# Layer two of a two-layer trunk: memory attention moved to its front, one sample step per pair of heads, twelve gates at its end

## The chip, the cores and the metric

The kernel runs on one core of a Trainium2 chip. The metric is the device time of one execution in microseconds (us). The median of three runs of the kernel before is 906.5 us (905.1 to 909.17).

## The reference, cut to what matters

One inference step of a two-layer decoder trunk of width 2048, for two groups of requests that share the weights: a prompt of 256 tokens and 8 samples of one token, so 264 columns in all. Layer one mixes tokens by sliding-window attention, layer two by a gated linear recurrence (HGRN2) with 12 heads of 128x128 state. Each layer also has 4 heads of attention over a memory of 256 rows, a SiLU gate over all 16 blocks of 128, an output projection and a LayerNorm.

```python
q, f, iv, mq, g = split(h @ w_in)                 # layer two: 12, 12, 12, 4, 16 blocks of 128
fg = lb + (1 - lb) * sigmoid(f);  k = 1 - fg;  q = silu(q)
S_t = fg_t * S_{t-1} + k_t v_t^T;  o_t = q_t S_t  # per head; S starts at 0 (prompt) or at the state (samples)
o = o * rsqrt(mean(o^2) + 1e-6) * norm_w
mem_o = softmax(mq @ mk^T / sqrt(128)) @ mv       # prompt: mk, mv computed here; samples: from caches
y = (concat(o, mem_o) * silu(g)) @ w_out
h = LayerNorm(alpha * h + y)
```

The outputs are both hidden states, the memory keys and values, the window of keys and values, and the recurrent states of the prompt and of the 8 samples.

## The kernel before, in words

**Units.** The work is a list of some 170 units (class `Stream`, lines 58 to 131). A unit is one 128x2048 block of weights, cache or state in float32 (1 MB; a state unit of the kernel before has half of it) and a function that uses it. For each unit the block is loaded into one of four `raw` buffers by the sync engine's queue (`load`, line 79), then split into two float16 halves in one of four `hl` buffers: the high part by ScalarE (line 97), the low part by VectorE (line 98). Loads and splits run up to four units ahead. A block with `whole=True` keeps its `raw` buffer until its unit has run.

**Projections.** `proj` (line 308) multiplies a unit's block with the 264 columns: 16 chunks of 128 rows, three float16 passes each (lines 303 to 305), 48 matmuls of 264 columns into a PSUM bank of tag `pj`, of which there are two. The result is read out of its bank by ScalarE and VectorE, and only then the bank is free for a later projection.

**Layer two before.** For each pair of heads the units are f, f, v, v, then for each head q, half a block of sample state, and for heads 0 to 7 the gate. Then come the four memory queries mq, eight cache units c_mk and c_mv with gates 8 to 13 between, the other gates, and the 16 output projections o.

**Side steps.** When the second q of a pair is projected, `hq_unit` (line 1009) hands the pair to a generator, `hg_side` (line 1064), which goes on one step after each unit: `after(i)` calls `pump(1)`. A pair's chain computes scores in levels of 1, 2, 4, ..., 64 tokens. `prepare` (ScalarE line 1079, VectorE lines 1080, 1084 and 1087) makes the operands of a level, `products` the matmuls hs, `keep` (line 1111) copies them under a mask. After level 64 come the copy of its scores (1147), the transposes pk (1152) with the copy kn (1154), the state product pu (1158), the output hpo (1169 to 1171), its copy osb (1173), squares (1177), the row means rms (1182), Ln and Exp with a table load each (1183, 1186), and the scaled output (1189). A gate that was projected early lies in `mix` and is multiplied in at once (`gate_by`, lines 728 to 730); otherwise `gate_unit` does so when its turn comes, and pumps the chain until the head is done. The memory heads have such generators too (`memp_side`).

**Sample state.** `state_unit` (line 1197) computes a head's sample outputs from the split state (matmuls hos), then updates the float32 state in its `raw` buffer: matmuls vb spread the values over partitions, ScalarE scales by the forget gate (line 1237, 8 times a head), VectorE adds (line 1238), and the buffer is written back as out_ss by GpSimd's queue.

**Order.** The code is written for a tile framework that places the instructions of each engine in one order, by its own estimate of when each could start; each engine then runs its row strictly in that order, waiting on semaphores. PSUM tags matter for it: `pj` two banks, `pt` two (pk, pu, vb and the transposes hvp and hvr), `sc` two (hs, rms), `pv` and `ms` one each. `hvt`, the copy of a pair's v, has one buffer.

Of the kernel before, what the change touches and what calls it, by code (L numbers as in the profile page):

```python
# [18 lines left out]
P = 128  # L19
NC = 16  # L20
# [13 lines left out]
NG1 = 8  # L34
# [23 lines left out]
class Stream:  # L58


    def __init__(self, nc, pool, nraw, nsplit):
        self.nc, self.pool = nc, pool
        self.nraw, self.nsplit = nraw, nsplit
        self.units = []
        self.raw = {}
        self.hl = {}

# [37 lines left out]
    def run(self, pump):  # L105
# [11 lines left out]
        for i in range(n):  # L117
# [8 lines left out]
            while free < prepped and (free <= i or self.units[free][5]):  # L126
                free += 1
# [7 lines left out]
def trunk_kernel(  # L135
# [75 lines left out]
    bias_s = pm.tile([P, 2, NQ], F32, name="bias_s")  # L211

# [770 lines left out]
    def f_unit(h):  # L983
        def fn(hl):
# [4 lines left out]
            pt = proj(hl, xhl, T, f"f{h}")  # L989
            i = h % 2  # L990
            if i == 0:
# [3 lines left out]
                cur["ks8"] = p1.tile([P, 2, TS], F32, tag="ks8", name=f"ks8{h}", bufs=2)  # L995
            fg, kk, ks8 = cur["fg"][:, i], cur["kk"][:, i], cur["ks8"][:, i]
# [6 lines left out]
            nc.vector.tensor_scalar_mul(ks8, kk, 1.0 / (SA * SK))  # L1003
# [5 lines left out]
    def hq_unit(h):  # L1009
        def fn(hl):  # L1010
# [5 lines left out]
            if h % 2 == 1:  # L1016
                side.append(hg_side(h // 2, cur["q"], cur["vn"], cur["fg"], cur["qk"]))
# [23 lines left out]
    def hv_rows(h, vt, vs, vn, vr):  # L1041
# [7 lines left out]
        nc.vector.tensor_copy(vr[:, i], p16)  # L1049
# [14 lines left out]
    def hg_side(pi, q, vn, fg, qk):  # L1064
# [119 lines left out]
        for i, sq in enumerate(sqs):  # L1184
# [3 lines left out]
            scaled = mix[:, h] if h >= NG1 else sq  # L1188
# [3 lines left out]
            if h < NG1:  # L1192
                gate_by(sq, mix[:, h], h)
# [3 lines left out]
    def state_unit(h):  # L1197
        def fn(hl):
            p1 = H["p"]
            pi, i = h // 2, h % 2  # L1200
            raw = stream.raw[state_at[h]][:, : TS * P]
            R = raw.rearrange("p (b v) -> p b v", b=TS)
            v = hl[:, :, : TS * P].rearrange("p s (b v) -> p s b v", b=TS)
            vr, fgs, ks8 = cur["vr"][:, i], cur["fg"][:, i, TP:T], cur["ks8"][:, i]
            qs, vts = (cur[n][:, i, TP:T] for n in ("q", "vt"))
            ks = cur["kk"][:, i]
            if i == 0:
                osb[pi] = p1.tile([P, 2, T], F32, tag="osb", name=f"osb{pi}", bufs=2)
            qk = p1.tile([P, TS], F32, tag="qk", name=f"qk{h}", bufs=2)
# [5 lines left out]
            nc.scalar.activation(qkh[:, 0], qk, AF.Copy)
            nc.vector.tensor_tensor(qkh[:, 1], qk, qkh[:, 0], op=ALU.subtract)
            nc.scalar.activation(qfh[:, :, 0], qf, AF.Copy)
            nc.vector.tensor_tensor(qfh[:, :, 1], qf, qfh[:, :, 0], op=ALU.subtract)
            po = bank("ms", 1, f"hos{h}")
            pov = po[:, : 2 * TS].rearrange("p (b s) -> p b s", s=2)  # L1220
            for b in range(TS):
                mm(pov[:, b], v[:, 0, b], qfh[:, b], start=True, stop=False)
                mm(pov[:, b, 0:1], v[:, 1, b], qfh[:, b, 0:1], start=False, stop=True)
            pq = po[:, 2 * TS : 3 * TS]
# [48 lines left out]
    while late:  # L1273
        g1(late.popleft())
# [158 lines left out]
```

## Time and profile before

| | |
|---|---|
| runs | 905.1, 906.5, 909.17 us; median 906.5 |
| the profiled execution | 906.08 us |
| its span, first to last instruction | 904.3 us |
| mean granted TensorE clock | 0.994 |
| TensorE, VectorE, ScalarE busy | 98%, 78%, 64% |
| HBM | 180.03 MB read, 17.22 MB written, 218 GB/s over the span |

All durations in this text are from that one execution. PE is TensorE, PEld its weight load, DVE VectorE, ACT ScalarE, POOL GpSimd, SP the sync engine; L303 is line 303 of the kernel. The chain of waits follows the work that ended last backwards; in the rows of groups the columns are busy time, mean nanoseconds of one instruction, and the idle time of the engine before them with what ended it. By the first and last start of their matmuls, f of layer two begins at 420.1 us, the last hq is at 701.7, the memory queries end at 729.2, the sample memory attention (mso) at 783.3, the gates at 799.8, and the output projections at 893.1.

### The profile page before, as it was taken

To read this page: it belongs to the slowest core of one execution; us is meant where nothing else is said; L and a number is where in the kernel's file an instruction comes from. 1 tells how busy PE (TensorE), PEld (TensorE's weight loads), DVE (VectorE), ACT (ScalarE), POOL (GpSimd) and SP (SyncE) were. 2 spreads that over 40 slices of the span, in tenths; PEclk is the share of its full clock that TensorE was granted. 3 is DMA by queue.
4 is the path that set the end of the run, shared out by engine and by line. 5 is a ranking of instruction groups with operands and counts; after the bars stand their busy time and mean duration, and the time that the engine had idled before them with its cause. 6 is when DMAs were issued, how large, how long until landed. Compare 5 with 4: busy or idle time off the path is not lost.

```text
span 904.3 us, 21814 instructions
## 1 busy us (share of the span) xinstructions
PE 886.6 (98%) x9281; PEld 762.9 (84%) x9281; DVE 701.5 (78%) x1230; ACT 582.4 (64%) x982; POOL 34.9 (4%) x68
## 2 busy tenths in 40 slices
PE   9999999999999999999999999999999999799996
PEld 6888889678888888876888888898888888688996
DVE  6879877669886666697687887979788989678736
ACT  6767776657664444476766877777777585858415
POOL 1100010000000000002000000000000000000000
PEclk9999999999999999999999999999999999899999
DMA  9998566557785555556374655827454878456303
GB/s 340 392 353 317 188 245 209 188 208 265 262 333 192 187 192 203 207 198 214 127 292 137 216 201 174 299 101 260 160 215 164 303 283 308 172 207 244 130 2 97
DMA packets 37853, 198.67 MB, mean 220 GB/s; under 512 B 4555, under 2 KB 10732, under 8 KB 17532
## 3 DMA queue, kind: packets, MB, share of 16 engines
q1 hardware_dynamic: 33024, 181.55, 56.3%
q0 software_dynamic: 4688, 15.67, 4.6%
q8 instruction: 72, 1.18, 0.5%
q14 instruction: 25, 0.20, 0.1%
q10 hardware_dynamic: 44, 0.07, 0.0%
HBM read 180.03 MB, written 17.22 MB: 218 GB/s over the span
## 4 chain that ended last, share of the span: by engine, by line
PE 77%; DVE 8%; ACT 6%; DMA 6%; issue 3%; SPq 0%; ACTq 0%; DVEq 0%
PE o L303 5%; PE o L305 5%; PE o L304 5%; PE g L305 5%; PE g L303 5%; PE g L304 5%; DVE hl L98 4%; ACT hl L97 2%; PE hv L305 2%; PE hv L303 2%; PE hv L304 2%; DMA raw<-in_w_in 2%; PE hq L303 2%; PE hq L305 2%; PE hq L304 2%
## 5 line engine op out<-in xcount | busy, mean ns | idle before, releaser
L98 DVE SCALAR_TENSOR_TENSOR hl<-raw,hl 128x2048 f16<-128x2048 f32 (+2 forms) x168 | 358.6, 2138 | 82.0 <-ACT hl L97 81.0
L97 ACT ACTIVATE hl<-raw 128x2048 f16<-128x2048 f32 (+2 forms) x168 | 299.2, 1784 | 97.8 <-PE o L305 45.4
L305 PEld LDWEIGHTS <-hl 128*128 128x128 f16 (+2 forms) x2048 | 197.4, 98 | 31.8 <-DVE hl L98 2.9
L303 PEld LDWEIGHTS <-hl 128*128 128x128 f16 (+2 forms) x2048 | 197.3, 98 | 30.6 <-issue 2.2
L304 PEld LDWEIGHTS <-hl 128*128 128x128 f16 (+2 forms) x2048 | 197.4, 98 | 30.3 <-issue 2.2
L305 PE MATMUL g<-xhl,hl 128*128 128x264 f16 x512 | 142.0, 277 | 2.4 <-DVE hl L98 2.4
L303 PE MATMUL g<-xhl,hl 128*128 128x264 f16 x512 | 141.9, 277 | 0.0
L304 PE MATMUL g<-xhl,hl 128*128 128x264 f16 x512 | 141.9, 277 | 0.0
L303 PE MATMUL o<-mix,hl 128*128 128x264 f16 x384 | 105.4, 276 | 0.8 <-DVE xres L747 0.8
L304 PE MATMUL o<-mix,hl 128*128 128x264 f16 x384 | 105.8, 276 | 0.0
L305 PE MATMUL o<-mix,hl 128*128 128x264 f16 x384 | 105.7, 276 | 0.0
L303 PE MATMUL q<-xhl,hl 128*128 128x264 f16 x192 | 53.0, 276 | 1.0 <-DVE kst L251 1.0
L303 PE MATMUL f<-xhl,hl 128*128 128x264 f16 x192 | 52.9, 276 | 0.4 <-DVE mvhl L251 0.4
L305 PE MATMUL hv<-xhl,hl 128*128 128x264 f16 x192 | 53.0, 276 | 0.0
L303 PE MATMUL hq<-xhl,hl 128*128 128x264 f16 x192 | 53.0, 276 | 0.0
L304 PE MATMUL hq<-xhl,hl 128*128 128x264 f16 x192 | 53.0, 276 | 0.0
L305 PE MATMUL hq<-xhl,hl 128*128 128x264 f16 x192 | 53.0, 276 | 0.0
L304 PE MATMUL hv<-xhl,hl 128*128 128x264 f16 x192 | 53.0, 276 | 0.0
L303 PE MATMUL hv<-xhl,hl 128*128 128x264 f16 x192 | 53.0, 276 | 0.0
L304 PE MATMUL q<-xhl,hl 128*128 128x264 f16 x192 | 53.0, 276 | 0.0
L305 PE MATMUL q<-xhl,hl 128*128 128x264 f16 x192 | 53.0, 276 | 0.0
L304 PE MATMUL f<-xhl,hl 128*128 128x264 f16 x192 | 52.9, 276 | 0.0
(338 smaller groups left out, 1858.4 us busy)
## 6 DMA issues: line engine op xcount, KB each, us to landing
raw<-in_w_in SPq DMA_DIRECT2D x88, 1024.0 KB, 6.4
raw<-in_w_o SPq DMA_DIRECT2D x32, 1024.0 KB, 5.0
raw<-in_w_mk SPq DMA_DIRECT2D x8, 1024.0 KB, 4.9
raw<-in_w_mv SPq DMA_DIRECT2D x8, 1024.0 KB, 4.9
raw<-in_c_mk SPq DMA_DIRECT2D x8, 1024.0 KB, 5.1
raw<-in_c_mv SPq DMA_DIRECT2D x8, 1024.0 KB, 7.0
raw<-in_state SPq DMA_DIRECT2D x12, 512.0 KB, 5.4
out_ss<-raw POOLq DMA_DIRECT2D x12, 512.0 KB, 5.5
```

The costliest lines, as they stand in the source:

```text
L97: hi = self.nc.scalar.activation(hl[:, 0, s], raw[:, s], AF.Copy, scale=scale)
L98: lo = self.nc.vector.scalar_tensor_tensor(hl[:, 1, s], raw[:, s], scale, hl[:, 0, s], op0=ALU.mult, op1=ALU.subtract)
L303: mm(out, lhs(0), rhs(0), start=start, stop=False)
L304: mm(out, lhs(0), rhs(1), start=False, stop=False)
L305: return mm(out, lhs(1), rhs(0), start=False, stop=stop)
```

## The change

The list of units of layer two is written anew.

- The four memory queries come right behind f of head 0, then the eight cache units, each with one projection of pair 0 (or gates 0 and 1, or f of pair 1) behind it.
- A pair's two half state units become one of 1 MB, for both heads. The small operations on it are joined (128x16 in place of 128x8), the update of its second head is put off to the next unit (`later`), and the stream holds its `raw` buffer one unit longer (`longer`).
- From pair 2 on a pair has seven units: f, f, v, v, q, q, state; gate 2 follows pair 1's state, gate 6 that of pair 3. Only gates 0, 1, 2 and 6 are early. The other twelve are last, with those of heads 10 and 11 at the very end, ahead of the output projections.
- `after` pumps no step behind a cache unit, two behind f of head 1 and v of head 0, one behind f of head 2, else one, or two where more than one generator is waiting (after state unit 0).
- `apart=True`: q of head 0 in layer one and f of head 0 in layer two use the `pv` bank and do all passes with high weights first.
- The constant `sel` carries the factor 1/(SA*SK), so the multiply into ks8 (line 1003 before) is gone.
- `LATER` is empty: the code for late state updates (`fetch`, `late_update`, `with_update`, `kept`) never runs.

What the engines' rows become at three places follows. Line numbers of the new kernel are a few higher (L307 to L309 are the passes, L1088 and L1092 in `prepare`, L1213 the scaling).

TensorE, pair 3's last levels, before: hs3_64 is level 64 of pair 3, hv9 and hq8 are projections of heads 9 and 8.

```order
L305 MATMUL hv9_8935<-xhl_93,hl123_8684 128x264
...
L303 MATMUL hs3_64_8987<-qk16_2_5655 128x64
...
L303 MATMUL hq8_9018<-xhl_93,hl124_8779 128x264
...
L304 MATMUL hs3_64_8987<-qk16_2_5655 128x64
...
L1152 MATMUL pk3_9001<-ident_66,qk32_6_7952 128x128 x4
L1045 MATMUL hvp8_9008<-ident_66,hvt8_8897 128x128 x2
...
L305 MATMUL hq8_9018<-xhl_93,hl124_8779 128x264
...
L1158 MATMUL pu3_9070<-vn6_8108,kn3_9006 128x128 x4
```

The same place now:

```order
L309 MATMUL hv11_9894<-xhl_93,hl134_9732 128x264
...
L308 MATMUL hs3_4_9152<-qk16_3_5656 128x64
...
L307 MATMUL hs3_16_9302<-qk16_0_5653 128x64
...
L307 MATMUL hs3_64_9395<-qk16_2_5655 128x64
...
L1160 MATMUL pk3_9409<-ident_66,qk32_6_8310 128x128 x4
L1053 MATMUL hvp9_9416<-ident_66,hvt8_9239 128x128 x2
L1177 MATMUL hpo3_9488<-st3_8947,vn6_8505 128x128
...
L1166 MATMUL pu3_9477<-vn6_8505,kn3_9414 128x128 x4
...
L307 MATMUL hq10_9960<-xhl_93,hl135_9737 128x264
```

Before, parts of hv9 and hq8 stood between the levels and behind pk; now levels 4 to 64 and the rest of the chain follow one another, and the next projection, hq10, stands behind pu.

ScalarE around the same levels, before (raw125 is a state, 16x16 is level 16):

```order
L1079 ACTIVATE qk16_3_5656<-qk32_6_7952 128x2x32x8
...
L97 ACTIVATE hl125_8843<-raw125_8591 128x1024
...
L1079 ACTIVATE qk16_0_5653<-qk32_6_7952 128x2x16x16
L1237 ACTIVATE raw125_8591<-raw125_8591,fg8_8738 128x128 x8
L1079 ACTIVATE qk16_1_5654<-qk32_6_7952 128x2x8x32
```

Now (raw137 is the state of pair 5):

```order
L100 ACTIVATE hl137_9891<-raw137_9672 128x2048
L1087 ACTIVATE qk16_3_5656<-qk32_6_8310 128x2x32x8
L1213 ACTIVATE raw137_9672<-raw137_9672,fg10_9658 128x128 x16
L1087 ACTIVATE qk16_0_5653<-qk32_6_8310 128x2x16x16
L100 ACTIVATE hl138_9957<-raw138_9735 128x2048
L1087 ACTIVATE qk16_1_5654<-qk32_6_8310 128x2x8x32
```

Eight scalings behind the step of level 16 have become sixteen ahead of it.

TensorE at the end of pair 5, before: g113 and g114 are gates, mso and msc the memory attention.

```order
L305 MATMUL g113_10980<-xhl_93,hl151_10791 128x264
...
L305 MATMUL hs5_64_10507<-qk16_2_5655 128x64
L1152 MATMUL pk5_10521<-ident_66,qk32_10_9379 128x128 x4
...
L1171 MATMUL hpo5_10636<-qk32_10_9379,s15_10570 128x128
L677 MATMUL mback1_10698<-ident_66,mrows1_10690 128x32 x2
L1182 MATMUL rms50_10704<-osq50_10644,ones_rms_81 128x264
L1182 MATMUL rms51_10707<-osq51_10646,ones_rms_81 128x264
...
L696 MATMUL mso1_10796<-msphl1_10701,hl148_10576 128x2
...
L303 MATMUL msc10_10774<-mkhl_97,mqhl_96 128x256
```

And now: o10 and o11 are output projections 0 and 1 of layer two; behind the rms rows they go on with chunk 10, which is head 10's.

```order
L309 MATMUL o11_0_11229<-mix_95,hl151_11038 128x264
...
L309 MATMUL hs5_64_10744<-qk16_2_5655 128x64
L1160 MATMUL pk5_10758<-ident_66,qk32_10_9659 128x128 x4
...
L1179 MATMUL hpo5_10896<-qk32_10_9659,s15_10830 128x128
L1190 MATMUL rms50_10968<-osq50_10904,ones_rms_81 128x264
L1190 MATMUL rms51_10971<-osq51_10906,ones_rms_81 128x264
...
L307 MATMUL o10_0_11171<-mix_95,hl150_10978 128x264
```

The gates have moved ahead of the chain's last steps, and the memory attention has left the place.

The diff, cut to its core:

```diff
-NG1 = 8
+EARLY = (0, 1, 2, 6)
+LATER = ()
...
-            while free < prepped and (free <= i or self.units[free][5]):
+            while free < prepped and (free + self.longer.get(free, 0) <= i or self.units[free][5]):
...
+        if apart:
+            pt = bank("pv", 1, name)
+            for k, (c, s, r) in enumerate([(c, 0, r) for c in range(NC) for r in range(2)] + [(c, 1, 0) for c in range(NC)]):
+                mm(pt[:, :n], w[:, s, c], src[:, r, c, cols], start=k == 0, stop=k == 3 * NC - 1)
+            return pt[:, :n]
...
-            nc.vector.tensor_scalar_mul(ks8, kk, 1.0 / (SA * SK))
...
+    def update(h, R, vr, fgs, ks, sel):
+        for g in range(2):
+            pvb = bank("pt", 2, f"vb{h}{g}")
+            for bb in range(4):
+                mm(pvb[:, bb * P : (bb + 1) * P], sel[:, 4 * g + bb], vr, start=True, stop=True)
+            for bb in range(4):
+                b = 4 * g + bb
+                s = R[:, b]
+                nc.scalar.activation(s, s, AF.Copy, scale=fgs[:, b : b + 1])
+                nc.vector.scalar_tensor_tensor(
+                    s, pvb[:, bb * P : (bb + 1) * P], ks[:, b : b + 1], s, op0=ALU.mult, op1=ALU.add
+                )
+        nc.gpsimd.dma_start(ss_o[h // 2, :, h % 2 * TS * P : (h % 2 + 1) * TS * P], R.rearrange("p b v -> p (b v)"))
...
+            half(0)
+            later.append(lambda: half(1))
...
+    f_of(0)
+    for h in range(NM):
+        w1("mq", h, mem1_sides(mq_unit(h)) if h == NM - 1 else mq_unit(h))
+    cache(c_mk, ck_unit, 0)
+    f_of(1, 2)
...
+    for pi in range(2, HD // 2):
+        for of in (f_of, v_of):
+            of(2 * pi)
+            of(2 * pi + 1)
+        q_of(2 * pi)
+        q_of(2 * pi + 1)
+        state_of(pi)
+        if 2 * pi in EARLY:
+            gate_of(2 * pi)
...
-        pump(1)
+        pump(pumps[i] if i in pumps else 2 if len(side) > 1 and i > state_at[0] else 1)
...
-        sel[b, b] = 1
-        sel[TS + b, b] = 1
+        sel[b, b] = 1 / (SA * SK)
+        sel[TS + b, b] = 1 / (SA * SK)
```

More of the change, by code (lines that the diff above doesn't have):

```diff
@@ L988, in fn @@
             p1 = H["p"]
-            pt = proj(hl, xhl, T, f"f{h}")
+            pt = proj(hl, xhl, T, f"f{h}", apart=h == 0)
             i = h % 2
@@ L1201, in fn @@
[L1201 to L1209, printed above, removed]
@@ L1215, in fn @@
[L1215 to L1223, printed above, removed]
@@ L1224, in fn @@
-            pq = po[:, 2 * TS : 3 * TS]
+            qkh = p1.tile([P, 2, 2, TS], F16, tag="qkh", name=f"qkh{pi}", bufs=2)
+            split_from(qfh[:, :, :, 0], qfh[:, :, :, 1], qf, 1.0)
+            split_from(qkh[:, 0], qkh[:, 1], qk, 1.0)
+            po = bank("ms", 1, f"hos{pi}")
+            pov = po[:, : 4 * TS].rearrange("p (i b s) -> p i b s", i=2, s=2)
+            for i in range(2):
+                for b in range(TS):
+                    mm(pov[:, i, b], v[:, 0, i, b], qfh[:, i, b], start=True, stop=False)
+                    mm(pov[:, i, b, 0:1], v[:, 1, i, b], qfh[:, i, b, 0:1], start=False, stop=True)
@@ new lines, in fn, with half, w1, state_of @@
+            R = raw.rearrange("p (i b v) -> p i b v", i=2, b=TS)
+            def half(i):
+                update(2 * pi + i, R[:, i], vr[:, i, : P // 2].bitcast(F16), fgs[:, i], ks[:, i], H["sel"])
+            half(0)
+            later.append(lambda: half(1))
+        return fn
+    state_at, pumps = {}, {}
+    def w1(part, i, fn, n=None):
+        if n is not None:
+            pumps[len(stream.units)] = n
+        stream.add(wb(w_in1, NB1[part] + i), fn)
+    def state_of(pi):
+        at = state_at[pi] = len(stream.units)
+        whole = 2 * pi not in LATER
+        if whole:
+            stream.longer[at] = 1
+        stream.add(state[pi], state_unit(pi), SA, whole=whole)
@@ L1259, in mem1_sides, with gate_of, cache @@
+    def gate_of(h, n=None):
+        w1("g", h, early_gate(h) if h in EARLY else gate_unit(1, h), n)
+    def cache(c, unit, t):
+        pumps[len(stream.units)] = 0
+        stream.add(c[1, t], unit(1, t), SA)
     def mem1_sides(fn):
         return with_side(fn, [lambda h=h: memp_side(1, h) for h in range(NM)])
-    u = stream.units[-1]
-    stream.units[-1] = (u[0], mem1_sides(u[1]), *u[2:])
-    def g1(j):
-        stream.add(wb(w_in1, NB1["g"] + j), gate_unit(1, j))
-    late = deque(range(NG1, NC))
@@ L1269, in trunk_kernel, with f_of, v_of, q_of @@
-    for n, (c, unit, t) in enumerate([(c_mk, ck_unit, t) for t in range(4)] + [(c_mv, cv_unit, t) for t in range(4)]):
-        stream.add(c[1, t], unit(1, t), SA)
-        if late and (late[0] < NQ or n == 7 or late[0] < NQ + 2 and n > 3):
-            g1(late.popleft())
-    while late:
-        g1(late.popleft())
+    def f_of(h, n=None):
+        w1("f", h, f_unit(h), n)
+    def v_of(h, n=None):
+        w1("v", h, hv_unit(h), n)
+    def q_of(h, n=None):
+        w1("q", h, hq_unit(h), n)
@@ new lines, in trunk_kernel, with fetch_first, f @@
+    v_of(3)
+    q_of(2)
+    q_of(3)
+    state_of(1)
+    gate_of(2)
+    for pi in range(2, HD // 2):
[7 more added lines that the diff above has]
+            gate_of(2 * pi)
+    last = (HD - 2, HD - 1)
+    def fetch_first(fn):
+        def f(hl):
+            for h in LATER[:3]:
+                fetch(h)
+            fn(hl)
+        return f
+    for k, j in enumerate([j for j in range(NC) if j not in EARLY and j not in last] + list(last)):
+        w1("g", j, fetch_first(gate_unit(1, j)) if k == 6 else gate_unit(1, j))
```

123 lines of the change are left out of this document (80 added, 43 removed).

## The prediction

> **What bounds the kernel now.** I read the page first: busy time, then the slices.
>
> ```profile
> span 904.3 us, 21814 instructions
> ...
> PE 886.6 (98%) x9281; PEld 762.9 (84%) x9281; DVE 701.5 (78%) x1230; ACT 582.4 (64%) x982; POOL 34.9 (4%) x68
> ...
> PE   9999999999999999999999999999999999799996
> ...
> PEclk9999999999999999999999999999999999899999
> ```
>
> TensorE is busy for 98% of the span, and one slice only, the 35th (769 to 791 us), shows both a 7 and a clock of 8. The matmuls that both kernels issue are nearly the same, so the change can only win or lose where TensorE stands still. Then the windows by stage:
>
> ```profile
> 420.00:720.00 300.00, 299.64 (x3172) 265.32 (x3172) 246.97 (x477) 217.29 (x387) 13.62 (x25) 1.00 0.58 205
> ...
> 760.00:800.00 40.00, 34.50 (x394) 28.69 (x392) 32.70 (x54) 27.56 (x48) 0.54 (x1) 0.91 0.62 230
> ```
>
> The columns are length, then busy time of TensorE, its weight load, VectorE, ScalarE and GpSimd, then the granted clock, the DMA share and GB/s. From 420 to 720, where pairs 0 to 4 of the recurrence run among projections, TensorE loses 0.36 us of 300. From 760 to 800 it is idle for 40 - 34.50 = 5.5 us, and the clock of 0.91 costs about 40 x 0.09 = 3.6 us more: 9.1 us. TensorE's rows in order of time (start, length) place it, and the chain of waits through the window (the same columns) says why:
>
> ```profile
> 763.58 0.28 PE L303 MATMUL g<-xhl,hl 128*128 128x264 f16 x1
> 763.69 0.28 PE L304 MATMUL g<-xhl,hl 128*128 128x264 f16 x1
> ...
> 769.25 0.19 PE L304 MATMUL hs<-qk 128*128 128x64 f16 x1
> 769.28 0.19 PE L305 MATMUL hs<-qk 128*128 128x64 f16 x1
> 769.31 0.63 PE L1152 MATMUL pk<-ident,qk 128*128 128x128 f32 x4
> 771.47 0.49 PE L1169 MATMUL hpo<-st,vn 128*128 128x128 f32 x2 [1.53 <-ACT st L1147]
> ...
> 774.35 0.39 PE L1171 MATMUL hpo<-qk,s 128*128 128x128 f32 x2
> ...
> 776.01 0.71 PE L1182 MATMUL rms<-osq,ones_rms 128*128 128x264 f32 x2
> ```
>
> ```profile
> 775.02 0.48 ACT osb L1173
> 775.53 0.73 ACT osq L1177 x2
> ...
> 776.41 1.28 ACT L1183
> 777.71 0.85 ACT osq L1183 x2
> ...
> 779.87 0.43 ACT osq L1186
> 780.33 0.90 DVE mix L1189 x2
> ...
> 785.43 0.40 PE g L305
> ```
>
> This is the end of the last pair's chain (pair 5, heads 10 and 11): transposes, state product, squares, two table loads around Ln and Exp, then the scaled output. It runs while the memory softmax has its own chain, and little projection work is left between.
>
> **What the change takes away.** The memory units move ahead of the pairs, and the twelve gates fill the time of the last chains; the 9.1 us of that place go. Two more waits are aimed at, by `apart` for q0 and f0:
>
> ```profile
> L303 PE MATMUL q<-xhl,hl 128*128 128x264 f16 x192 | 53.0, 276 | 1.0 <-DVE kst L251 1.0
> L303 PE MATMUL f<-xhl,hl 128*128 128x264 f16 x192 | 52.9, 276 | 0.4 <-DVE mvhl L251 0.4
> ```
>
> I count both as gone, 1.4 us, and 0.3 for the small matmuls that joining the state steps saves (twelve, at most the 0.03 us that hs matmuls start apart). The dropped ks8 multiply and the joined small steps save VectorE and ScalarE a few us, spread over a stretch where neither ends a wait of TensorE: nothing. Removed in all: 9.1 + 1.4 + 0.3 = 10.8 us. If the cover of the memory chain failed in its new place, the 1.0 us wait of L677 and its like would come back there.
>
> **What it adds.** Three places in the new order have TensorE run into a chain with no projection between. The prices come from these groups of layer two (420 to 800 us; busy time and mean ns of one, then the idle time before), VectorE's, then ScalarE's, and from a state's load on the page (us from issue to landing):
>
> ```profile
> L98 DVE SCALAR_TENSOR_TENSOR hl<-raw,hl 128x2048 f16<-128x2048 f32 (+1 forms) x76 | 161.3, 2123 | 23.0 <-ACT hl L97 22.5
> L1080 DVE TENSOR_TENSOR qk<-qk,qk 128x512 f16<-128x512 f32 x42 | 29.2, 695 | 9.3 <-ACT qk L1079 9.2
> ...
> L1084 DVE TENSOR_TENSOR qk<-qk,prod 128x512 f32<-128x512 f32 x36 | 24.8, 689 | 0.4
> L1111 DVE COPY_PREDICATED st<-mask_t,hs 128x256 f32<-128x256 int32 x36 | 19.1, 531 | 0.6 <-PE hs L305 0.5
> ...
> L730 DVE TENSOR_TENSOR mix<-osq,mix 128x264 f16<-128x264 f32 x8 | 3.2, 429 | 0.4
> L728 DVE SCALAR_TENSOR_TENSOR osq<-osq,mix 128x264 f32<-128x264 f32 x8 | 3.2, 428 | 0.0
> ```
>
> ```profile
> L97 ACT ACTIVATE hl<-raw 128x2048 f16<-128x2048 f32 (+1 forms) x76 | 134.5, 1770 | 21.9 <-DMA raw<-in_w_in 6.7 <-PE g L305 5.3 <-issue 3.8
> L1237 ACT ACTIVATE raw<-raw,fg 128x128 f32<-128x128 f32 x96 | 29.5, 391 | 3.5 <-DVE hl L98 3.5
> L1079 ACT ACTIVATE qk<-qk 128x512 f16<-128x512 f32 x42 | 27.4, 653 | 21.2 <-DVE qk L1084 17.1 <-DVE qk L1121 4.0
> ...
> L1034 ACT ACTIVATE hvt<-hv 128x264 f32<-128x264 f32 x12 | 4.5, 379 | 6.8 <-PE hv L305 6.8
> L1046 ACT ACTIVATE vn<-hvp 128x256 f32<-128x256 f32 x12 | 4.5, 377 | 0.0
> ...
> L1154 ACT ACTIVATE kn<-pk 128x512 f32<-128x512 f32 x6 | 3.5, 591 | 0.4 <-PE pk L1152 0.3
> ...
> L729 ACT ACTIVATE mix<-osq 128x264 f16<-128x264 f32 x8 | 3.1, 418 | 3.0 <-DVE osq L728 3.0
> ...
> L1147 ACT ACTIVATE st<-hs 64x256 f32<-64x256 f32 x6 | 2.2, 370 | 1.9 <-PE hs L305 1.9
> ```
>
> ```profile
> raw<-in_state SPq DMA_DIRECT2D x12, 512.0 KB, 5.4
> ```
>
> A projection of one head is 48 matmuls that start 0.11 us apart in the rows above, some 5.4 us; hs matmuls start 0.03 us apart, 12 to a level, 0.35 us.
>
> *Place A, pair 5 and the first output projections.* In the order TensorE does nothing after pair 5's two rms matmuls but output projections o10 and o11 from their chunk 10 on, and chunk 10 is head 10's gated output. Both pj banks are held, so o12 cannot slip in. From the last hpo matmul to L1189 for head 10 the rows above give 780.8 - 774.7 = 6.1 us; gating adds L728, L729, L730: 1.3; the second head's copies between, 0.4; less 0.7 for the rms matmuls: 7.1 us idle. Before it, pk to hpo waited 1.53 with ScalarE behind a weight split; without that split I take 1.0, and 0.3 for pu. So 8.4 us, and after a stop of 7 us the clock, which was 0.91 round the present stop, takes some 1.6, a little under half of the 3.6 us lost there: 10 us; bounds 8 (no clock loss) and 12 (both waits and the full 3.6 us that the present clock loss came to).
>
> *Place B, pair 3, between hv11 and hq10.* TensorE has hs3_4, hs3_16, hs3_64, pk3 and hq10 in a row. Of these, hs3_16 and hs3_64 wait for VectorE. Its queue from the end of hs3_4 to the step that hs3_64 needs is four L1111 (2.1), four L1080 (2.8), two L1084 (1.4) and one weight split (2.1): 8.4 us, less 0.7 for hs3_16: 7.7. That is the low side. ScalarE is worse: its sixteen L1237 of state 5 (16 x 29.5 / 96 = 4.9 us) now stand ahead of the L1079 that level 16 needs. They follow the state's split, which starts when hv10 is done and frees its hl buffer: 1.77 + 2.12 = 3.9 us later the scales begin, they end at 8.8, L1079 at 9.5, and from there VectorE has L1080, L1084, the split, two L1080, L1084, two L1111, L1080: 7.3 us, so hs3_64 starts at 16.8 where TensorE has 5.4 + 0.7 + 0.7 = 6.8 us of work: 10.0 idle. With 1.0 for pk to hpo: 11. Bounds: 7.7 + 1.0 = 8.7, and 16 if the state's load is late by as much as a landing (5.4 us on the page), since each state now holds a 1 MB buffer longer and its write-back starts a unit later. I take 11, the in-order sum; I add no clock loss, which is in the high end.
>
> *Place C, pair 1, between hv7 and hq6.* The same arithmetic: state 3's split ends 3.9 us after hv6, its scales at 8.8, then a weight split (10.6), L1147 (10.9), L1154 (11.5), hvp's copy, hvt and the small split that frees a pj bank (L1046, L1034 and about 0.3 for two of 128x8): 11.5 + 0.38 + 0.38 + 0.3 = 12.6, against 5.4 + 1.8 = 7.2 us of work. 5.4 idle; I take 5, bounds 1.5 (the hpo wait of 1.53 alone, if the scales start earlier) and 7.
>
> Pairs 0, 2 and 4 have projections between all levels (f4 and f5, hv8 to hq9, g15 to g112): no price. The cache units run beside pair 0's projections, two loads to a projection; in layer one cache units also sit among projections, and I see no stop there.
>
> Sum: the profiled execution took 906.1 us, 1.8 more than its span and 0.4 under the median of 906.5. 906.1 - 10.8 + 10 + 11 + 5 = 921.3; forecast 921. Its own range: 906.1 - 10.8 + 8 + 8.7 + 1.5 = 913.5 to 906.1 - 10.8 + 12 + 16 + 7 = 930.3.
>
> **Two rules weighed.** The clock round the present stop was 0.91 over 40 us. The Trainium skill, "TensorE: Matmul & The Clock Gate", Part 1, says that an idle window of about 3.4 us puts the clock at half until a busy window has passed. This trace agrees in size: 3.6 us lost in two such dips. By that rule place B would cost an estimated 1.7 more, and the sum would be 923.
> TensorE lost 0.36 us of 300 among the pairs. The Trainium skill, "Perfetto Trace Analysis", Optimization Strategy, reads a repeating gap as too few buffers in SBUF or PSUM. No run here shows such a gap yet; B and C, with both pj banks held, would be ones.
>
> **The rivals.**
> *Only A is real.* VectorE is idle for 53 of the 300 us and ScalarE for 83, so levels of pairs 1 and 3 may be ready sooner than I sum. Against it: the order leaves no cover there. 906.1 - 10.8 + 10 = 905.3: no change. Chance 0.15.
> *Faster: the gates hide the chain.* If the chains run so far ahead that B and C vanish and o10 meets chunk 10 after only the present 1.53 us wait twice, 906.1 - 10.8 + 3.1 = 898.4. It decides at A: below about 6 us there, with nothing at B and C, the kernel is faster. For it: 299.64 of 300 busy with the same chains. Against it: seven units a pair from pair 2 on where there are ten now for pairs 0 to 3. Chance 0.24.
> *The cache units wait for loads.* Sixteen 1.05 MB loads stand among eight projections of 5.4 us plus about 0.4 each: 16.8 MB in 46 us is 365 GB/s.
>
> ```profile
> GB/s 340 392 353 317 188 245 209 188 208 265 262 333 192 187 192 203 207 198 214 127 292 137 216 201 174 299 101 260 160 215 164 303 283 308 172 207 244 130 2 97
> ```
>
> The best slice reached 392, the next 353; at 330 the stage takes 51 us, 5 more, on top of the forecast: 926. Chance 0.09.
>
> **How the numbers follow.** The forecast has 0.52. About 0.5%, 4.5 us, is what a measurement of this kernel can tell from no change. Slower: 0.52 + 0.09 = 0.61; same: 0.15; faster: 0.24. The range reaches from 896, under the faster rival, to 929, near the forecast's high end; some of both tails is left out.
>
> **What would show it.** Right: TensorE idle 7 to 9 us before an o row with mix as releaser; a gap of about 10 us between hv and hq matmuls with hs waiting for VectorE L1088 in pair 3; one of about 5 in pair 1; no stop in the memory stage. Wrong: a full TensorE row between the first f and the last g, or waits for `raw` loads there.

## The result and the profile after

The changed kernel took 927.15 us (median of 4 runs, 924.62 to 928.69), the kernel before 906.26 (905.1 to 909.17): a ratio of 1.0224, 95% interval 1.0207 to 1.0242. It is slower by 20.9 us. The forecast was 921 and slower; the value lies in its range of 896 to 929, near the top. The profiled execution took 927.33 us at a mean clock of 0.984 (before: 906.08 at 0.994).

Page of the changed kernel, busy times and slices:

```profile
span 925.6 us, 21690 instructions
...
PE 892.8 (96%) x9269; PEld 766.9 (83%) x9269; DVE 696.7 (75%) x1170; ACT 580.7 (63%) x964; POOL 35.0 (4%) x68
...
PE   9999999999999999999999999989996999979996
...
PEclk9999999999999999999999999989997999989999
```

Where before had one dip of both rows, there are now three: slices 27, 31 and 36, which begin at 601, 694 and 810 us. The span grew by 925.6 - 904.3 = 21.3 us. TensorE's idle time went from 904.3 - 886.6 = 17.7 to 925.6 - 892.8 = 32.8, so 15.1 of the 21.3 are idle time. The other 6.2 are matmuls that took longer, although there are twelve fewer of them.

The windows by stage (length, then busy time of TensorE, its weight load, VectorE, ScalarE and GpSimd, then clock, DMA share, GB/s):

```profile
420.00:600.00 180.00, 178.34 (x1982) 157.33 (x1981) 142.14 (x216) 130.97 (x215) 8.31 (x15) 1.00 0.65 234
600.00:650.00 50.00, 45.58 (x468) 40.01 (x466) 37.81 (x72) 33.31 (x60) 1.61 (x3) 0.93 0.48 180
650.00:760.00 110.00, 100.26 (x1050) 88.34 (x1048) 85.74 (x154) 73.59 (x128) 3.21 (x6) 0.94 0.49 181
760.00:800.00 40.00, 39.57 (x399) 34.69 (x397) 34.60 (x66) 24.57 (x34) 1.61 (x3) 1.00 0.59 214
800.00:850.00 50.00, 43.60 (x396) 36.80 (x395) 30.97 (x43) 27.55 (x34) 0.54 (x1) 0.93 0.41 146
```

The stop of before at 760 to 800 is gone: 0.43 us of idle time where 5.5 had been; the end of pair 5's chain, which made it, now lies at 800 to 850. Idle now are 4.42 us in 600 to 650, 9.74 in 650 to 760 and 6.40 in 800 to 850, and each of these three has a clock of 0.93 or 0.94. TensorE's rows that had to wait there, in order of time (start, length, and in brackets the idle time before and what ended it), name the places:

```profile
613.81 0.80 PE L1177 MATMUL hpo<-st,vn 128*128 128x128 f32 x2 [4.42 <-ACT st L1155]
...
708.39 0.23 PE L307 MATMUL hs<-qk 128*128 128x64 f16 x1 [4.07 <-ACT qk L1087]
709.12 0.21 PE L308 MATMUL hs<-qk 128*128 128x64 f16 x1 [0.49 <-DVE qk L1088]
...
710.71 0.23 PE L307 MATMUL hs<-qk 128*128 128x64 f16 x1 [0.85 <-ACT qk L1087]
713.12 0.21 PE L308 MATMUL hs<-qk 128*128 128x64 f16 x1 [2.17 <-DVE qk L1088]
715.00 0.24 PE L307 MATMUL hs<-qk 128*128 128x64 f16 x1 [1.14 <-ACT qk L1087]
715.74 0.21 PE L308 MATMUL hs<-qk 128*128 128x64 f16 x1 [0.50 <-DVE qk L1088]
...
822.39 0.49 PE L1179 MATMUL hpo<-qk,s 128*128 128x128 f32 x2 [0.47 <-ACT s L1170]
...
824.69 1.16 PE L1190 MATMUL rms<-osq,ones_rms 128*128 128x264 f32 x4 [1.14 <-ACT osq L1185]
...
830.63 0.60 PE L307 MATMUL o<-mix,hl 128*128 128x264 f16 x2 [4.78 <-ACT mix L738]
```

These are the forecast's places C (state product of pair 1, behind `st`), B (levels 16 to 64 of pair 3) and A (the output projections, at head 10's `mix`), in that order of time. At B the waits add up to 9.22 us. The chain of waits through 700 to 720 of the changed kernel shows why:

```profile
700.72 2.29 DVE hl L101
...
703.04 1.61 ACT raw L1213 x6
...
704.81 3.01 ACT raw L1213 x10
707.82 0.52 ACT qk L1087
708.34 1.81 ACT hl L100
...
710.17 2.29 DVE hl L101
712.47 1.25 DVE qk L1088 x2
713.71 0.57 DVE qk L1092
714.28 0.36 DVE st L1119
```

A split on VectorE (L101) releases the sixteen scalings of state 5 on ScalarE (L1213); the step of level 16 (L1087) stands behind them; behind that a split on each of the two engines. From the first scaling to level 64's last wait it is 715.74 - 703.04 = 12.7 us; the forecast's in-order sum had 16.8 - 3.9 = 12.9.

At C the chain of waits is of the same kind: the split of state 3 on both engines, its sixteen scalings, a weight split, and only then the copy `st` (L1155) for which `hpo` waits at 613.81.

```profile
602.64 1.92 ACT hl L100
...
604.59 2.30 DVE hl L101
...
606.91 1.32 ACT raw L1213 x5
...
611.70 1.80 ACT hl L100
613.49 0.28 ACT st L1155
```

The clock round the stops, in windows of the changed kernel laid from the moment it falls to the moment it is back (C, then B, then A; in the 3.4 us ahead of each and behind each it is 1.00):

```profile
612.21:619.03 6.82, 5.22 (x24) 4.40 (x25) 4.09 (x9) 3.46 (x9) 0.55 (x1) 0.50 0.30 96
707.78:721.43 13.65, 7.88 (x59) 6.72 (x60) 8.28 (x14) 6.52 (x14) 0.00 (x0) 0.50 0.21 79
827.25:834.07 6.82, 3.44 (x16) 2.26 (x16) 2.37 (x6) 2.67 (x5) 0.00 (x0) 0.50 0.00 0
```

TensorE has work without a break from 613.81, 715.74 and 830.63 on, so 5.2, 5.7 and 3.4 us of steady work behind the stops ran at half speed. With the short matmuls between B's waits, TensorE was busy for 5.22, 7.88 and 3.44 us at half clock, and half of that is lost: 2.6, 3.9 and 1.7 us, 8.3 in all. The three stretches are two, four and two times 3.41 us long. Counted in such steps, the clock was back at each stop behind the first step in which TensorE was busy throughout; where work sets in within a step, the rest of that step is slow as well.

### The profile page after: what moved, and what is told of

Same layout as the page of the kernel before. It is cut to its first block, busy times and chain, and to the rows that moved or that the text cites. A ratio compares the mean times of both kernels' runs of the same rounds, so it can differ in the third digit from the quotient of the medians.

```text
span 925.6 us, 21690 instructions
## 1 busy us (share of the span) xinstructions
PE 892.8 (96%) x9269; PEld 766.9 (83%) x9269; DVE 696.7 (75%) x1170; ACT 580.7 (63%) x964; POOL 35.0 (4%) x68
## 4 chain that ended last, share of the span: by engine, by line
PE 88%; ACT 5%; DVE 5%; issue 1%; DMA 0%; ACTq 0%
PE o L307 6%; PE o L308 6%; PE o L309 6%; PE g L307 6%; PE g L309 6%; PE g L308 6%; DVE hl L101 2%; PE hq L307 2%; PE hq L309 2%; PE hq L308 2%; PE q L308 2%; PE q L309 2%; PE q L307 2%; ACT hl L100 2%; PE f L307 2%; PE f L309 2%
## 5 line engine op out<-in xcount | busy, mean ns | idle before, releaser
L101 DVE SCALAR_TENSOR_TENSOR hl<-raw,hl 128x2048 f16<-128x2048 f32 (+2 forms) x162 | 357.5, 2211 | 93.0 <-ACT hl L100 92.4
L100 ACT ACTIVATE hl<-raw 128x2048 f16<-128x2048 f32 (+2 forms) x162 | 297.9, 1843 | 90.6 <-PE o L309 47.9
L307 PEld LDWEIGHTS <-hl 128*128 128x128 f16 (+2 forms) x2016 | 194.6, 98 | 34.4 <-issue 6.1
L308 PEld LDWEIGHTS <-hl 128*128 128x128 f16 (+2 forms) x2016 | 194.7, 98 | 29.8 <-issue 1.3
L309 PEld LDWEIGHTS <-hl 128*128 128x128 f16 (+2 forms) x2016 | 194.6, 98 | 28.6 <-issue 0.2
L307 PE MATMUL g<-xhl,hl 128*128 128x264 f16 x512 | 141.4, 276 | 0.4 <-DVE sil L743 0.4
L309 PE MATMUL g<-xhl,hl 128*128 128x264 f16 x512 | 141.4, 276 | 0.0
L307 PE MATMUL o<-mix,hl 128*128 128x264 f16 x384 | 106.5, 278 | 4.8 <-ACT mix L738 4.8
L309 PE MATMUL o<-mix,hl 128*128 128x264 f16 x384 | 106.6, 278 | 0.0
L307 PE MATMUL hq<-xhl,hl 128*128 128x264 f16 x192 | 53.9, 281 | 0.0
L308 PE MATMUL hq<-xhl,hl 128*128 128x264 f16 x192 | 53.7, 280 | 0.0
L309 PE MATMUL hq<-xhl,hl 128*128 128x264 f16 x192 | 53.6, 279 | 0.0
L309 PE MATMUL hv<-xhl,hl 128*128 128x264 f16 x192 | 53.0, 276 | 0.0
L307 PE MATMUL hv<-xhl,hl 128*128 128x264 f16 x192 | 53.0, 276 | 0.0
L308 PE MATMUL q<-xhl,hl 128*128 128x264 f16 x176 | 48.6, 276 | 0.0
L309 PE MATMUL q<-xhl,hl 128*128 128x264 f16 x176 | 48.6, 276 | 0.0
L307 PE MATMUL q<-xhl,hl 128*128 128x264 f16 x176 | 48.6, 276 | 0.0
L309 PE MATMUL f<-xhl,hl 128*128 128x264 f16 x176 | 48.6, 276 | 0.0
L308 PE MATMUL f<-xhl,hl 128*128 128x264 f16 x176 | 48.6, 276 | 0.0
```

The costliest lines, as they stand in the source:

```text
L100: hi = self.nc.scalar.activation(hl[:, 0, s], raw[:, s], AF.Copy, scale=scale)
L101: lo = self.nc.vector.scalar_tensor_tensor(hl[:, 1, s], raw[:, s], scale, hl[:, 0, s], op0=ALU.mult, op1=ALU.subtract)
L307: mm(out, lhs(0), rhs(0), start=start, stop=False)
L308: mm(out, lhs(0), rhs(1), start=False, stop=False)
L309: return mm(out, lhs(1), rhs(0), start=False, stop=stop)
```

## The experiments

Three theories of the stops stood against each other. The first: buffers hold the cover back, since both `pj` banks and the single `hvt` buffer are held and the next projection cannot start. The second: ScalarE's order, the sixteen scalings of a state ahead of a chain's step. The third: the chains start too late. The six pairs' chains follow one another, and with the memory units in front of it pair 0's chain begins later; what it loses, the last pairs lack in projections. All edits are made on the changed kernel and each is compared with the kernel before, whose medians in the four sets were 907.11 (hvt2, pool_scale, gates_back, all_three), 906.94 (early_q1, two_steps, early_and_two, no_scale), 906.33 (pair0_first, pair0_first_two) and 905.61 (outs_spread, pair0_first_outs). Idle times are those of the windows 600 to 650, 650 to 760 and 800 to 850, where C, B and A lie in the changed kernel; in some kernels other waits stand in them.

**hvt2**: a second `hvt` buffer, paid for with one of `s2`.

```diff
-tag="vt", name=f"hvt{h}", bufs=1)
+tag="vt", name=f"hvt{h}", bufs=2)
-tag="s2", name=f"s2{pi}", bufs=2)
+tag="s2", name=f"s2{pi}", bufs=1)
```

> One edit to the changed kernel: the copy hvt of a pair's v gets a second buffer (paid for by one buffer less of s2). Theory 1 (TensorE stops because both pj banks hold v projections that wait for hvt, so no projection can cover the chain): with the second buffer hq6 stands between levels 16 and 64 of pair 1 and hq10, hq11 and g13 among the levels of pair 3, so the stop at pair 1 (7.5 us) goes and that at pair 3 (14.0) falls to 4 or less; pair 5's chain moves later and loses all its cover from level 4 on, so the stop at the output projections (9.4) grows by about 10. Time about 920 us. Theory 2 (the sixteen scalings of the joined state ahead of the levels on ScalarE make the stops, whatever projection stands near): the stops at pairs 1 and 3 stay within 2 us, and with the longer one at the end the time is about 937.

Measured 920.35, ratio 1.0143 [1.0116, 1.0169]. Windows of this kernel:

```profile
600.00:650.00 50.00, 48.81 (x516) 42.94 (x515) 39.87 (x74) 35.25 (x64) 1.61 (x3) 1.00 0.57 203
650.00:760.00 110.00, 105.76 (x1116) 92.57 (x1115) 88.63 (x159) 76.79 (x131) 3.21 (x6) 0.98 0.53 194
...
800.00:850.00 50.00, 40.97 (x345) 33.91 (x344) 30.94 (x40) 28.44 (x32) 0.54 (x1) 0.86 0.40 145
```

C falls from 4.42 us of idle time to 1.19, B from 9.74 to 4.24, and A grows from 6.40 to 9.03. The buffer has a part in C and B; 2.6 of the 8.7 us that it saves come back at A. The first theory, whose time was 920, holds for a part: some 13 us against before are left.

**pool_scale** and **no_scale**: the state scalings on GpSimd, and not at all.

```diff
-nc.scalar.activation(s, s, AF.Copy, scale=fgs[:, b : b + 1])
+nc.gpsimd.tensor_scalar_mul(s, s, fgs[:, b : b + 1])
```

In no_scale the line is left out.

> One edit to the changed kernel: the sixteen scalings of a state go from ScalarE to GpSimd. TensorE's row changes with it: pair 1's end has projections between its steps again, pair 3 has 3.5 us of projection between levels 4 and 16 and none after, pair 5 has 2.7 around pk. Theory 2 (the scalings on ScalarE): the stop at pair 1 goes (7.5), that at pair 3 falls from 14.0 to 5 to 7, that at the end by 2: 910 us. Theory 1 (cover and banks alone): pair 1 goes, pair 3 falls by the 3.5 us of cover to 10, the end by 2: 914. Rival 3 (GpSimd is too slow for it, or disturbs VectorE): state write-backs come late, loads wait for their buffers, 925 or more.

> The changed kernel without the scaling of the sample states by the forget gate (sixteen ScalarE instructions per pair; the states written back then lack the decay). TensorE's row is that of the kernel with the scalings on GpSimd. Theory 2: as there the stop at pair 1 is gone; what GpSimd's 1.03 us a scaling cost in late write-backs is gone as well, and pair 3 falls to 5 or less: 908 to 911 us. Theory 1 or 3 (pair 3's stop is lacking cover, VectorE's queue between its levels): pair 3 keeps 10 or more and the time stays at 915 to 918, as with GpSimd.

Measured 917.3, ratio 1.0115 [1.0087, 1.0143], and 914.89, 1.009 [1.0065, 1.0115]. Windows of no_scale, the second round its stop at B:

```profile
650.00:760.00 110.00, 101.40 (x1067) 89.56 (x1065) 88.59 (x163) 66.63 (x97) 3.22 (x6) 0.95 0.48 176
...
690.00:716.00 26.00, 19.66 (x183) 17.30 (x180) 17.35 (x41) 11.72 (x22) 1.61 (x3) 0.80 0.23 86
```

C is gone in both. At B some 6.3 us of waits stay, where the changed kernel had 9.22, with no scaling in the program at all; 2.3 more, at the start of pair 4's chain, bring the window to 8.6 (8.73 with the scalings on GpSimd). The second theory fails as the whole cause of B: without the scalings the next work in the queue sets the time. Either edit also changes the order on TensorE, so the share of ScalarE's time alone is not told apart. In time, no_scale lies at the lower edge of the 915 to 918 expected for a lack of cover; pool_scale is a miss, 3 us above the first theory's 914 and well under the 925 of late write-backs.

**gates_back**: gates 3, 4, 5 and 7 go back among the pairs.

```diff
-EARLY = (0, 1, 2, 6)
+EARLY = (0, 1, 2, 3, 4, 5, 6, 7)
...
+    gate_of(3)
...
-        if 2 * pi in EARLY:
-            gate_of(2 * pi)
+        for h in (2 * pi, 2 * pi + 1):
+            if h in EARLY:
+                gate_of(h)
```

> One edit to the changed kernel: gates 3, 4, 5 and 7 go back behind the pairs (eight early gates, eight at the end), nine units a pair for pairs 1 to 3. Theory 1 (cover): pairs 1 and 3 have projections among all levels again; pair 3 lacks them only from level 64 to pu, so the 14.0 us at pair 3 become about 5 and the 7.5 at pair 1 go; but pair 5's levels 4 to 64 and its end now follow one another with nothing between, and the 9.4 us there become about 20. 921 us. Theory 2 (scalings on ScalarE): stops at pairs 1 and 3 shrink by less than a third, the end grows: 930 or more. If the number of gates at the end did not matter, the end would stay at 9.4 and the time would be 910.

Measured 921.94, ratio 1.0167 [1.0138, 1.0196], as the first theory expected. Idle time is 0.61, 5.92 and 8.89 us in the three windows. The waits among pair 3's levels are covered; most of the 5.92 is a stop of C's kind, now at pair 3's state product:

```profile
724.98 0.80 PE L1177 MATMUL hpo<-st,vn 128*128 128x128 f32 x2 [4.64 <-ACT st L1155]
```

The four gates that stand among the pairs are missed at the end.

**all_three**: hvt2, pool_scale and the two steps of two_steps (below) together.

> The changed kernel with three edits together: scalings on GpSimd, two hvt buffers, and two steps behind every unit once the first state unit is past (not only under backlog). TensorE's row has projections among all levels of all pairs but the last steps of pair 1 (pk to rms) and pair 2 and 3's last step. Theory 1 and 2 alike: stops of 5 to 6 us at pair 1, 1 to 2 at pairs 2 and 3, and 6 at the output projections, where only Ln, Exp and the gating are left uncovered: 927 - 34 + 14 = 907 us, about the kernel before. If GpSimd's scalings delay write-backs, loads of weights stop TensorE between the pairs: 915 or more.

Measured 920.1, ratio 1.0129 [1.0087, 1.0172]: a miss, by 13 us from the lower value and on the side that the expectation named for late GpSimd scalings. Idle time was 6.80, 4.48 and 2.77 in the three windows. In its trace TensorE waits twice, 2.7 us in all, for a bank that VectorE's state updates (L1214) hold, a wait that the changed kernel does not have; the rest is spread. Remedies that each shorten a wait do not add up.

**early_q1**, **two_steps** and **early_and_two**: q of head 1 right behind q of head 0, which lets pair 0's chain begin a few projections earlier; two steps behind every unit once the first state unit is past; and both.

```diff
-    gate_of(0)
+    q_of(1)
...
-    gate_of(1)
+    gate_of(0)
...
-    q_of(1)
+    gate_of(1)
```

```diff
-        pump(pumps[i] if i in pumps else 2 if len(side) > 1 and i > state_at[0] else 1)
+        pump(pumps[i] if i in pumps else 2 if i > state_at[0] else 1)
```

> One edit to the changed kernel: q of head 1 moves from behind cache unit c_mv 1 to right behind q of head 0, gates 0 and 1 each go one cache unit later; so the chain of pair 0 can start two projections (11 us) earlier, and as the chains of the six pairs follow each other without a gap (a pair's hd starts where the one before has its rms), all of them with it. Theory 3 (the row of chains, started late and paced by units, is the resource that runs short, and the stops lie where the order runs out of projections): pair 1's end has 3 us of projections between its steps and its stop (7.5) goes, pair 3 has cover between levels 4 and 16 but none after, so 14.0 falls to 6 to 8; the end stays at 9. Time 912 us. If the start of the chains does not matter, 925 or more.

> One edit to the changed kernel: two steps of the front chain behind every unit after the first state unit, not only where two chains are waiting. Theory 3: pair 3's levels have projections between them, its 14.0 us go; but pairs 1 and 2 now crowd their last steps (nothing between pk, pu and rms), so pair 1 keeps 7 to 9 and pair 2 gets 2, and pair 5 loses its cover between levels 16 and 64, 12 in place of 9. Time 919 us. If pacing only moved stops about, 925 to 930.

> Both edits on the changed kernel: q of head 1 two projections earlier, two steps behind every unit after the first state unit. TensorE's row then has projections among all levels of all pairs and among the last steps of all but pair 3 (hpo to rms, 2 us); at the output projections gate 11, o10 and o11 stand among pair 5's last steps, and only Ln, Exp and gating are left, 5 to 6 us. Theory 3: the stops of 31 us (9.4 + 14.0 + 7.5) shrink to 8 or 9, 904 us, at or under the kernel before. Theory 1 (pj banks and the one hvt buffer, which both stay): stops at pairs 1 and 3 stay in part, 912 or more.

Measured 916.19, ratio 1.0105 [1.0075, 1.0135]; 927.03, 1.0223 [1.0188, 1.0257]; and 907.97, 1.0014 [0.9999, 1.0028]. Idle time in the three windows: 0, 8.80 and 5.70; then 6.02, 6.37 and 6.89; then 0.37, 4.50 and 3.33. A faster pace alone gains nothing and was a miss, 8 us above its 919: the waits among pair 3's levels are gone, but C stays and others come up behind the levels of pairs 2 and 3. The earlier start gains 11 us, and with it the same pace gains another 8. Both are nearer to the third theory's values (912 and 904) than to the others (925 and 912), and 4 us above them.

**pair0_first**: the whole of the third theory. Pair 0's f, v, q and state units stand ahead of the memory projections; behind the cache units stand gates 0 and 1 and then pair 1's f, v and q, with one step each. Nothing else differs from the changed kernel.

```diff
+    f_of(1)
+    v_of(0)
+    v_of(1)
+    q_of(0)
+    q_of(1)
+    state_of(0)
     for h in range(NM):
...
-    f_of(1, 2)
+    gate_of(0, 1)
...
-    v_of(0, 2)
+    gate_of(1, 1)
```

> The changed kernel with the memory units moved behind pair 0 in place of ahead of it: f, f, v, v, q, q and the state of pair 0 first, then the four memory queries, then the eight cache units with gates 0 and 1 and the projections of pair 1 behind them, one step of a chain behind each. Nothing else changes (one hvt buffer, scalings on ScalarE, twelve gates last, two steps only under backlog). Theory 3 (the six chains in a row started too late): pair 0's chain starts some 40 us earlier; TensorE's row has projections among all levels and last steps of all six pairs, and o10 and o11 among pair 5's last steps; the stops at pairs 1 and 3 (7.5 and 14.0) and the small ones go, and of the 9.4 at the output projections 6 to 8 are left (Ln, Exp, gating): 900 to 902 us, under the kernel before by 5. If the memory units' place does not matter and the stops come from the seven units of a pair, the one hvt buffer or the joined state, 915 or more.

Measured 906.11, ratio 0.9997 [0.998, 1.0014]: from 927.15 back to the time of before, though 4 us above the 900 to 902 expected. Windows of this kernel:

```profile
600.00:650.00 50.00, 49.54 (x531) 43.57 (x530) 39.56 (x63) 38.17 (x66) 1.06 (x2) 1.00 0.64 231
650.00:760.00 110.00, 109.08 (x1159) 96.46 (x1157) 95.46 (x184) 79.28 (x136) 4.83 (x9) 1.00 0.58 204
...
800.00:850.00 50.00, 44.08 (x381) 37.37 (x379) 35.09 (x36) 32.75 (x32) 0.54 (x1) 0.93 0.48 178
```

C and B are gone, with one `hvt` buffer and with all scalings on ScalarE. The rows of the first product of each chain (`hd`, 8 matmuls to a pair; least, median and longest ns, then first and last start) show what moved, of the kernel before, the changed one and this one:

```profile
L1120 PE MATMUL hd<-hqs,qk x48: 272/275/275, 459.3 to 731.3; 128*128 128x128 f32 x48
```

```profile
L1128 PE MATMUL hd<-hqs,qk x48: 272/275/276, 490.1 to 783.5; 128*128 128x128 f32 x48
```

```profile
L1128 PE MATMUL hd<-hqs,qk x48: 272/275/275, 452.8 to 760.7; 128*128 128x128 f32 x48
```

The changed kernel starts its first chain 30.8 us after before's, and 37.3 after this one's. For the later chains the lead is smaller. Pair 1's first product starts at 570.5 us in the changed kernel, at 548.9 in early_q1, at 546.3 in early_and_two and at 546.5 in pair0_first; pair 3's at 683.5, 667.6, 659.6 and 660.1. The waits among pair 3's levels are 9.2, 7.5, 0 and 0.6 us. So the stop goes only with the last 8 us of the lead, and in early_and_two those come from the pace.

In TensorE's order, counted by the projections that stand within a chain, pair 0's chain has eleven in the changed kernel, and pair 3's five, from f10 to hq10; in pair0_first both have eight. What stands at B in the two (with the number of matmuls in a row), the changed kernel first:

```
hs3_4 x11, hv11 x8, hs3_4, hv11 x17, hs3_4 x11, hs3_16 x24, hs3_64 x12, pk3 x4, hvp9 x2, hpo3 x4, hvr9, pu3 x8, hq10
hs3_16 x11, hv10 x15, hs3_64, hv10 x19, hs3_64 x11, hv10 x6, hv11 x19, pk3 x4, hvp9 x2, hv11 x15, hpo3 x4, hv11 x5, hvr9, hv11, pu3 x8
```

That the place of the memory units causes C and B is thereby shown; that it does so by the late start of the chains is borne out by early_q1. It keeps the memory queries in front, only lets pair 0's chain begin earlier, and takes C and 0.9 us of B away. The `hvt` buffer has a share in the length of the stops, as hvt2 shows, and the scalings may have one. A, 5.92 us, is untouched, and one new wait of 1.65 us stands in the memory attention, at 524 us.

**pair0_first_two**: two steps behind each projection from pair 3's state on, on top of pair0_first.

```diff
-2 if len(side) > 1 and i > state_at[0] else 1)
+2 if len(side) > 1 and i > state_at[0] or i > state_at[3] else 1)
```

> The same with two steps behind every unit after the fourth state unit (pair 3's), not only under backlog. Theory 3: pair 5's chain ends a unit earlier, and 4 to 5 us in place of 6 to 8 are left at the output projections; pair 3's last steps are crowded as in the kernel with q of head 1 early and two steps, which cost 5 to 6 us there: 902 to 905 us, not better than one step.

Measured 908.14, ratio 1.0014 [0.9997, 1.0031], a miss: A falls to 2.77 us of idle time, and 4.92 stand in 650 to 760, 4.0 more than in pair0_first.

**outs_spread** and **pair0_first_outs**: o12 and o13 take the `pt` banks, and o10 to o13 take chunks 10 and 11 last, on the changed kernel and on pair0_first.

```diff
-        for c in range(NC):
-            passes(pt[:, :n], lambda s: w[:, s, c], lambda s: src[:, s, c, cols], c == 0, c == NC - 1)
+        for c in order:
+            passes(pt[:, :n], lambda s: w[:, s, c], lambda s: src[:, s, c, cols], c == order[0], c == order[-1])
...
-        pt = proj(hl, bhl, n, f"o{l}{i}_{cols.start}", cols, tag)
+        order = [c for c in range(NC) if c not in (HD - 2, HD - 1)] + [HD - 2, HD - 1] if l == 1 and i < 4 else range(NC)
+        pt = proj(hl, bhl, n, f"o{l}{i}_{cols.start}", cols, "pt" if l == 1 and i in (2, 3) else tag, order=order)
```

> The changed kernel with one edit at the output projections of layer two: o12 and o13 go into the two pt banks, which are free by then, and o10 to o13 take chunks 10 and 11 (heads 10 and 11) last, so that chunks 12 to 15 and the two further projections stand among pair 5's last steps and in front of the two chunks that wait. Theory 1 for place A (both pj banks held, so nothing can cover Ln, Exp and gating): the 9.4 us there fall to 1 or 2, and nothing else changes: 918 to 920 us. If the stop there has another cause (a late weight load, the clock), less than 4 us come off: 923 or more.

> The kernel with pair 0 ahead of the memory units, with the same edit at the output projections. Its 8.8 us at that place fall to 1 or 2, and with the stops at pairs 1 and 3 gone already the time is 898 to 900 us, under both kernels. If the place only passes the wait on (to o14 and the weights behind it, whose hl buffers come free later), 903 or more.

Measured 922.47, ratio 1.0184 [1.017, 1.0197], between its two values, and 899.85, ratio 0.9928 [0.9913, 0.9943], as expected. On the changed kernel the wait for `mix` falls from 4.8 to 0.8, but 2.7 us of waiting for weight splits (L100) come up behind it; pair0_first_outs, whose chain ends earlier, has none there. Windows of pair0_first_outs:

```profile
650.00:760.00 110.00, 109.10 (x1160) 96.51 (x1158) 95.11 (x184) 79.61 (x136) 4.83 (x9) 1.00 0.58 205
...
800.00:850.00 50.00, 50.00 (x504) 44.91 (x503) 38.45 (x46) 33.77 (x35) 0.31 (x1) 1.00 0.46 176
```

All three stops are gone, and this version is 0.7% under the kernel before. Banks and order were changed together; which of the two weighs more was not tried.

## Why the prediction was right, and which term was mis-sized

*What goes.* The 5.5 us stop of 760 to 800 went, all but 0.43. The waits of q and f went with `apart`; the groups of f0 and q0, which now come from line 316, have no idle time:

```profile
L316 PE MATMUL f<-xhl,hl 128*128 128x264 f16 x48 | 5.9, 276 | 0.0
...
L316 PE MATMUL q<-xhl,hl 128*128 128x264 f16 x48 | 5.6, 276 | 0.0
```

A small wait is new that the forecast had not: 420 to 600 now has 1.66 us idle where before had 0.36, and 1.5 of it is one `hvr` behind `vs`. What `apart` and the joined state steps are worth by themselves was not tried.

*Place A.* Forecast 8.4 us of idle time, measured 6.40. The 7.1 from the last hpo to `mix` came as 4.78 + 1.14 = 5.92; of the 1.3 ahead of it 0.47 came. Banks and order made the stop, as the forecast said: outs_spread and pair0_first_outs, which change both, took all but 0.8 us of that wait away.

*Place B.* Forecast 11, measured 9.74, by the queue that the forecast had summed. That sum gives the size in this order; no_scale shows that the scalings are at most a part of it. Of the 9.22 us of waits 6.06 end with ScalarE's step (L1087) and 3.16 with VectorE's (L1088), where the forecast's sign named VectorE alone.

*Place C.* Forecast 5, measured 4.42, again by the queue summed: from the start of the state's split to the end of `st` it is 613.77 - 602.64 = 11.1 us, where the sum had 10.9.

*The term that was too small is the clock.* The forecast said of B "I add no clock loss", and C got none; its start, that the change can win or lose only "where TensorE stands still", leaves out that the matmuls behind a stop run slower. The windows at half clock price it. The kernel before had two:

```profile
778.14:781.55 3.41, 3.31 (x41) 2.54 (x41) 1.22 (x3) 3.38 (x6) 0.00 (x0) 0.50 0.03 8
784.97:788.38 3.41, 2.94 (x14) 2.05 (x15) 3.41 (x7) 3.41 (x6) 0.00 (x0) 0.50 0.48 161
```

TensorE was busy for 3.31 + 2.94 us in them, so they cost 3.1 (forecast 3.6, which counted idle time too). In the changed kernel A cost 1.7 (forecast 1.6), and C and B 2.6 + 3.9 = 6.5 (forecast nothing). Of the 6.2 us by which TensorE's busy time grew, the clock is thus 8.3 - 3.1 = 5.2; the other 1.0 was not traced (forecast -0.3, for the small matmuls that went). The balance from the forecast: 921.3 + 6.5 + 0.1 + 0.5 + 1.3 less 2.4 of idle time (17.5 forecast net, 15.1 measured) = 927.3, against 927.33. The errors in idle time and in clock have opposite signs, so it is luck that the forecast came as near as it did.

The busy times of two kernels do not price one stop, even with the same 9269 matmuls. From pair0_first to pair0_first_outs it falls by only 885.0 - 883.1 = 1.9 us, because the stretch at A that goes (first row, 4.62 / 2 = 2.3 us) is partly made up for by a new one at the memory attention (second row, 1.7 us):

```profile
806.69:813.51 6.82, 4.62 (x22) 3.02 (x22) 2.36 (x6) 1.50 (x4) 0.00 (x0) 0.50 0.00 0
```

```profile
522.72:526.13 3.41, 3.41 (x31) 2.73 (x31) 3.41 (x4) 3.41 (x4) 0.00 (x0) 0.50 1.03 430
```

The Trainium skill, "TensorE: Matmul & The Clock Gate", Part 1, has the array at half clock after an idle window of about 3.4 us until one busy window of that length is over. At A the trace agrees, with 3.4 us of steady work at half clock; at C and B it was 5.2 and 5.7, as work set in within a step of 3.41 us, and at B the short matmuls between the waits ran at 0.50 too. The 923 that the prediction worked out by that rule pointed the right way and was too small.

*The rivals.* "Only A" fell: B and C are there. "Faster: the gates hide the chain" fell at all three places; its mechanism shows only where the chains run ahead. That pair0_first_outs, at 899.85, is near its 898.4 is partly chance, since that version also changes the output projections. "The cache units wait for loads" fell: from 420 to 500 TensorE lost 0.13 us.

```profile
420.00:500.00 80.00, 79.87 (x883) 70.21 (x882) 57.05 (x75) 52.03 (x75) 5.62 (x10) 1.00 0.66 239
```

*What the forecast did not say* is why pair 3 lacks cover. It argued from "seven units a pair from pair 2 on where there are ten now"; pair0_first keeps those seven and has no stop at B. What counts is how late pair 3's chain runs: when the first chain begins and, as early_and_two shows, at what pace the row goes on.

The Trainium skill, "Perfetto Trace Analysis", Optimization Strategy, says that a gap that repeats can mean too few buffers in SBUF or PSUM. hvt2 agrees for a part (C and B from 14.16 us to 5.43), and pair0_first, without the buffer, leaves 0.46 and 0.92: the order weighed more here.

## What to carry to other kernels

Where several dependent chains run one after another, start the first as early as its inputs allow, and count in the order how much independent work stands between the steps of the *last* ones; work put ahead of the first chain is paid for there. When a stop moves under every single remedy, look for what is late before it rather than at what it waits for. Price each stop of some 4 us or more with its clock loss too (1.7 to 3.9 us here), and let a consumer that needs a late input take that input last and leave a bank for those behind it.

## What the runs showed of the hardware that was not expected

The scaling of one 128x128 f32 block took 1035 ns on GpSimd and 387 on ScalarE. Rows of pool_scale and of the changed kernel:

```profile
L1213 POOL TENSOR_SCALAR raw<-raw,fg 128x128 f32<-128x128 f32 x96 | 97.7, 1035 | 156.0 <-DVE hl L101 137.1 <-DVE vs L255 18.8
```

```profile
L1213 ACT ACTIVATE raw<-raw,fg 128x128 f32<-128x128 f32 x96 | 28.8, 387 | 5.3 <-DVE hl L101 5.3
```

(Spans on GpSimd are rough in this profile.) Even so GpSimd's version cost only 917.3 - 914.89 = 2.4 us more than leaving the scalings out; the two were measured in different sets, and their intervals overlap. The write-back of a state landed 2.9 us after its issue in the changed kernel and 5.5 before, for the same 512 KB; why was not tried.

```profile
out_ss<-raw POOLq DMA_DIRECT2D x12, 512.0 KB, 2.9
```
